# A 3x3 convolution on one core: cutting one input load into 112 and four times 4 partitions, and merging stores

## The chip, the core and the metric

The kernel runs on one core of one Trainium2 chip. The metric is device time in microseconds (us) of one execution: 126.62 us before the change, the median of 3 runs (126.53 to 126.68). Lower is better.

## The reference, cut to what matters

```python
x: (16, 64, 64, 64) float32        # batch, c_in, h, w
weight: (128, 64, 3, 3) float32    # c_out, c_in, kh, kw
x_pad = np.pad(x, ((0, 0), (0, 0), (1, 1), (1, 1)))
for b, co, ci, kh, kw:
    output[b, co] += weight[co, ci, kh, kw] * x_pad[b, ci, kh:kh+h, kw:kw+w]
```

The output is (16, 128, 64, 64) in float32. So 16.8 MB of x and 0.3 MB of weights come in from device memory (HBM), and 33.6 MB go out.

## The kernel before

The 16 images are worked on in eight pairs. A pair fills all 128 partitions of the on-chip memory (SBUF): two images of 64 input channels, each partition holding one 64x64 channel, 16 KB. In the output a partition is one of 128 output channels, and a pair has two images of 16 KB on each partition.

One tensor `homes` has nine such 16 KB slots on every partition. `X_HOME` says in which slot the x of each pair stands, `O_HOME` in which two neighbouring slots its output is built; slots are used again and again, so a slot can be written only when what it held before has been read. Pair 7, for example, builds its output in slots 2 and 3, and pair 4 built its own in slots 3 and 4.

Every pair is done in two halves `h`. In each half GpSimd (POOL) forms sums and differences of image rows in half precision (lines 106, 113, 119), ScalarE (ACT) casts rows (line 124), TensorE (PE) multiplies them with transformed weights into four accumulators (line 162), ACT copies three of these out (line 182), and VectorE (DVE) and ACT combine them into the pair's output slots (lines 229 to 232). POOL works two halves ahead of PE.

All transfers are issued by one engine, SyncE (SP), in the order of the program (`keep`), and each waits there for its inputs; a later one cannot pass it. The order before:

1. The weights (line 58), x of pair 0 in two pieces, of pair 1 and of pair 2 (line 63), then x of pairs 3 and 4 in one transfer (line 72).
2. After the second half of a pair, its output (`store`). Pairs in `BOTH` go out as one transfer of 2 images x 16 KB per partition (line 190), the others as one transfer per image (line 199). `FEW = 5, 1, 7` makes an exception for the second image of pair 5: its first 57 rows go out over all 128 partitions, its last 7 rows in one transfer of 124 partitions and one of 4.
3. After the first half of pairs 2, 3 and 4, the load of x of pairs 5, 6 and 7 (line 63).

That makes 24 transfers. Each uses one of eight semaphores in turn, and a transfer waits until the one that used its semaphore before has landed.

The functions the diff touches:

Of the kernel before, what the change touches and what calls it, by code (L numbers as in the profile page):

```python
# [15 lines left out]
def kernel(  # L16
# [12 lines left out]
    nc = tc.nc  # L29
    B, CI, H, W = x.shape  # L30
    CO = weight.shape[0]
# [4 lines left out]
    keep = tc.keep_in_program_order  # L36
    x_rows = x.rearrange("b c h w -> (b c) h w")
# [10 lines left out]

    X_HOME = [0, 1, 2, 7, 8, 2, 7, 8]
    O_HOME = [5, 3, 0, 5, 3, 0, 5, 2]  # L50
    BOTH = (0, 3, 6)
    FEW = 5, 1, 7
    NEXT_LOADS = {(2, 0): 5, (3, 0): 6, (4, 0): 7}
    homes = slots.tile([128, 9, H, W], F32)
    xs = [homes[:, k, :, :] for k in X_HOME]
# [1 line left out]
    w_raw = const.tile([CO, CI * 9], F32)  # L57
    keep(nc.sync.dma_start(w_raw, w_flat))

    def load(p, cuts=((0, H),)):  # L60
        for lo, hi in cuts:
            keep(
                nc.sync.dma_start(
                    xs[p][:, lo:hi, :], x_rows[128 * p : 128 * p + 128, lo:hi, :]
                )
            )

    load(0, ((0, 34), (34, H)))
    load(1)
    load(2)  # L70
    rows = x_rows[128 * 3 : 128 * 5, :, :].rearrange("(g p) h w -> p g h w", g=2)
    keep(nc.sync.dma_start(homes[:, 7:9, :, :], rows))

# [113 lines left out]
    def store(p, both):  # L187
        if p in BOTH:
            pair = out[2 * p : 2 * p + 2, :, :, :].rearrange("b c h w -> c b h w")
            keep(nc.sync.dma_start(pair, both))  # L190
            return
        for b2 in range(2):
            parts = [(0, CO, 0, H)]
            if (p, b2) == FEW[:2]:
                at = H - FEW[2]
                parts = [(0, CO, 0, at), (0, 124, at, H), (124, 4, at, H)]
            for c, n, lo, hi in parts:
                keep(
                    nc.sync.dma_start(
                        out[2 * p + b2, c : c + n, lo:hi, :], both[c : c + n, b2, lo:hi, :]  # L200
                    )
                )

    for n, (p, h) in enumerate(halves):
        if n + 2 < len(halves):
            tr[halves[n + 2]] = transforms(nc.gpsimd, *halves[n + 2])
        if h == 0:
            both = homes[:, O_HOME[p] : O_HOME[p] + 2, :, :]
# [24 lines left out]
        if h == 1:  # L233
            store(p, both)
# [32 lines left out]
```

## Time and profile before

| | |
|---|---|
| median of 3 runs | 126.62 us |
| the profiled execution's own time | 126.84 us |
| its span, first to last instruction | 125.0 us |
| busy: PE, ACT, POOL, DVE | 77%, 65%, 72%, 51% |
| time of the packets of SP's queue, as a share of 16 DMA engines' span | 96.6% |
| bytes moved, mean rate | 50.77 MB, 406 GB/s |
| output transfers of one image: issue to landing, median | 16.7 us |
| output transfers of two images: issue to landing, median | 21.2 us |

How to read it: "busy" is the time in which an engine executes something, over the whole span. The 16 DMA engines carry the transfers in packets; a packet here is one row of one partition, mostly 16 KB, and a last packet of 4 bytes raises the semaphore. The trace has a record of every packet (start, length, bytes, but not which of the 16 engines carried it) and of every increment of a semaphore, so that one can see when each engine's share of a transfer has landed. Times below that are not of the page count from the first instruction of the span.

### The profile page before, as it was taken

Reading aid. Unit: us, or ns where it says so; the run is one execution under the profiler, and the core shown is the slowest. Engines: PE = TensorE matmul, PEld = TensorE weight load, DVE = VectorE, ACT = ScalarE, POOL = GpSimd, SP = SyncE. Lnnn points to the kernel's source line nnn. Section 1 sums busy time; section 2 is a strip of 40 time slices with the busy share of each in tenths; the row PEclk is TensorE's granted clock in tenths of the full one; section 3 lists DMA queues with packets and bytes.
Section 4 is the critical chain, followed back from the end, with each engine's and each line's share of the span. In section 5 each row is a group of like instructions: output and inputs, shape, how many; then the busy total and the mean of one; then the engine's idle time right before and its main releaser. Section 6 shows DMA issues by size and latency. Waiting matters only on the chain.

```text
span 125.0 us, 2161 instructions
## 1 busy us (share of the span) xinstructions
PE 96.3 (77%) x873; PEld 48.3 (39%) x873; DVE 64.3 (51%) x56; ACT 81.5 (65%) x86; POOL 90.5 (72%) x52
## 2 busy tenths in 40 slices
PE   0339999999999999999999999999999991000000
PEld 0213455554545545554545555545545540000000
DVE  0199484655738393947557483939374664000000
ACT  4456569789897979797888989797978842000000
POOL 2209999999999999999999999999999500000000
PEclk9999999999999999999999999999999999555555
DMA  4999999999999999999999999999999999999991
GB/s 126 364 433 440 430 430 430 425 346 404 430 425 419 440 430 440 406 425 425 432 438 398 430 425 425 435 430 425 430 419 428 428 421 431 435 425 440 430 388 63
DMA packets 3826, 50.77 MB, mean 406 GB/s; under 512 B 360, under 2 KB 488, under 8 KB 744
## 3 DMA queue, kind: packets, MB, share of 16 engines
q1 hardware_dynamic: 3816, 50.63, 96.6%
q8 instruction: 7, 0.11, 0.3%
q14 instruction: 3, 0.02, 0.1%
HBM read 17.07 MB, written 33.55 MB: 405 GB/s over the span
## 4 chain that ended last, share of the span: by engine, by line
PE 77%; DVE 3%; DMA 3%; POOL 1%; ACT 0%; issue 0%; DVEq 0%
PE acc L162 76%; DMA w_raw<-in_weight_dram 3%; DVE homes L231 1%; DVE ss L106 1%; POOL w L78 1%; DVE th L133 0%; DVE Wt L134 0%; PE wp L95 0%; ACT g0h L131 0%; DVEq L134 0%
## 5 line engine op out<-in xcount | busy, mean ns | idle before, releaser
L162 PEld LDWEIGHTS <-Wt 64*128 64x128 f16 x864 | 47.4, 96 | 50.0 <-issue 4.4
L182 ACT COPY ut<-acc 128x1024 f32<-128x1024 f32 x48 | 45.7, 1021 | 5.5 <-PE acc L162 5.5
L162 PE MATMUL acc<-xh,Wt 64*128 64x504 f16 (+3 forms) x384 | 46.9, 376 | 0.0
L106 POOL TENSOR_TENSOR ss<-homes 128x1024 f16<-128x1024 f32 x15 | 35.3, 2352 | 5.0 <-DMA homes<-in_x_dram 5.0
L229 DVE TENSOR_TENSOR homes<-acc,ut 128x1024 f32<-128x1024 f32 x16 | 19.6, 1225 | 32.4 <-PE acc L162 30.2
L119 POOL TENSOR_TENSOR ee<-homes 128x1024 f16<-128x1024 f32 x15 | 35.4, 2359 | 0.0
L162 PE MATMUL acc<-ss,Wt 64*128 64x504 f16 (+1 forms) x192 | 24.8, 392 | 2.4 <-DVE ss L106 2.4
L162 PE MATMUL acc<-ee,Wt 64*128 64x504 f16 (+1 forms) x192 | 26.3, 377 | 0.0
L232 ACT COPY homes<-acc 128x1024 f32<-128x1024 f32 x16 | 16.2, 1013 | 12.7 <-PE acc L162 12.0
L231 DVE TENSOR_TENSOR homes<-ut,acc 128x1024 f32<-128x1024 f32 x16 | 19.5, 1221 | 2.0 <-PE acc L162 1.3
L113 POOL TENSOR_TENSOR dd<-homes 128x512 f16<-128x512 f32 x15 | 20.0, 1332 | 0.0
L230 DVE TENSOR_TENSOR homes<-acc,ut 128x1024 f32<-128x1024 f32 x16 | 19.4, 1215 | 0.0
L124 ACT CAST xh<-homes 128x1088 f16<-128x1088 f32 x16 | 17.9, 1120 | 0.0
L162 PE MATMUL acc<-dd,Wt 64*128 64x504 f16 (+1 forms) x96 | 13.9, 392 | 0.0
L95 PE MATMUL wp<-ident,w 128*128 128x128 f16 x9 | 1.1, 309 | 4.8 <-POOL w L78 4.8
L133 DVE SCALAR_TENSOR_TENSOR th<-wp,g0h 128x384 f32<-128x384 f32 x1 | 0.6, 557 | 5.8 <-ACT g0h L131 5.8
L119 DVE TENSOR_TENSOR ee<-homes 128x1024 f16<-128x1024 f32 x1 | 2.9, 2866 | 0.0
L95 PEld LDWEIGHTS <-w 128*128 128x128 f16 x9 | 0.9, 158 | 4.7 <-POOL w L78 4.7
L78 POOL CAST w<-w_raw 128x576 f16<-128x576 f32 x1 | 0.7, 662 | 2.7 <-DMA w_raw<-in_weight_dram 2.7
L79 ACT CAST w<-w_raw 128x576 f16<-128x576 f32 x1 | 0.7, 671 | 1.9 <-DMA w_raw<-in_weight_dram 1.9
L79 ACT ACT_TABLE_LOAD x1 | 1.3, 1283 | 0.7 <-PEq L251 0.7
L106 DVE TENSOR_TENSOR ss<-homes 128x1024 f16<-128x1024 f32 x1 | 1.2, 1224 | 0.0
(15 smaller groups left out, 5.7 us busy)
## 6 DMA issues: line engine op xcount, KB each, us to landing
out_dram<-homes SPq DMA_DIRECT2D x9, 2048.0 KB, 16.7
out_dram<-homes SPq DMA_DIRECT2D x3, 4096.0 KB, 21.2
homes<-in_x_dram SPq DMA_DIRECT2D x5, 2048.0 KB, 19.0
homes<-in_x_dram SPq DMA_DIRECT2D x1, 4096.0 KB, 28.0
out_dram<-homes SPq DMA_DIRECT2D x1, 1824.0 KB, 22.6
homes<-in_x_dram SPq DMA_DIRECT2D x1, 1088.0 KB, 5.8
homes<-in_x_dram SPq DMA_DIRECT2D x1, 960.0 KB, 7.8
w_raw<-in_weight_dram SPq DMA_DIRECT2D x1, 288.0 KB, 3.2
```

The costliest lines, as they stand in the source:

```text
L79: keep(nc.scalar.copy(w16[:, 1, :], w_raw))
L95: keep(nc.tensor.matmul(wps[kh][:, k * CO : k * CO + CO], w16[:, :, 3 * kh + k :: 9], ident))
L106: keep(eng.tensor_add(t, v[:, j : j + 16, 0, :], v[:, j : j + 16, 1, :]))
L113: keep(eng.tensor_sub(t, v[:, j : j + RB, 1, :], v[:, j : j + RB, 0, :]))
L119: keep(eng.tensor_sub(t, xs[p][:, r - 1 : r + 15, :], xs[p][:, r + 1 : r + 17, :]))
L124: keep(nc.scalar.copy(t, xs[p][:, C_ROW[h] : C_ROW[h] + 17, :]))
L162: nc.tensor.matmul(tiles[:, b2, lo:hi, c_lo:c_hi], Wt[p0 : p0 + 64, wi, kw, :], src[p0 : p0 + 64, first : last + 1 : step, c_lo + kw - 1 : ...
L182: keep(nc.scalar.copy(ut, tiles))
L229: keep(nc.vector.tensor_add(ov[:, :, jg : jg + RB, 1, :], pg2, ug))
L230: keep(nc.vector.tensor_add(ov[:, :, jf : jf + RB, 0, :], pf1, uy))
L231: keep(nc.vector.tensor_sub(ov[:, :, jf : jf + RB, 1, :], ux, pf2))
L232: keep(nc.scalar.copy(ov[:, :, jg : jg + RB, 0, :], pg1))
```

## The change

Three things are altered, and nothing in the computation.

- The load of pair 2 (`FEW = 2, 112, 4`) goes as one transfer of partitions 0 to 111 and four transfers of 4 partitions each (112 to 115, 116 to 119, 120 to 123, 124 to 127), instead of one of 128.
- The second image of pair 5 goes out whole, over 128 partitions; the transfers of 57 rows, of 7 rows on 124 partitions and of 7 rows on 4 partitions are gone.
- `BOTH` has pairs 0, 1, 3, 4 and 6 instead of 0, 3 and 6, so pairs 1 and 4 go out by one transfer each instead of two.

It stays at 24 transfers. The order of the instructions on PE, DVE, ACT and POOL is the same as before.

```diff
-    BOTH = (0, 3, 6)
-    FEW = 5, 1, 7
+    BOTH = (0, 1, 3, 4, 6)
+    FEW = 2, 112, 4
...
-    def load(p, cuts=((0, H),)):
+    def load(p, cuts=((0, H),), parts=((0, 128),)):
         for lo, hi in cuts:
-            keep(
-                nc.sync.dma_start(
-                    xs[p][:, lo:hi, :], x_rows[128 * p : 128 * p + 128, lo:hi, :]
+            for c, n in parts:
+                at = 128 * p + c
+                keep(
+                    nc.sync.dma_start(
+                        xs[p][c : c + n, lo:hi, :], x_rows[at : at + n, lo:hi, :]
+                    )
                 )
-            )
...
-    load(2)
+    few = [(c, FEW[2]) for c in range(FEW[1], 128, FEW[2])]
+    load(FEW[0], parts=[(0, FEW[1])] + few)
...
         for b2 in range(2):
-            parts = [(0, CO, 0, H)]
-            if (p, b2) == FEW[:2]:
-                at = H - FEW[2]
-                parts = [(0, CO, 0, at), (0, 124, at, H), (124, 4, at, H)]
-            for c, n, lo, hi in parts:
-                keep(
-                    nc.sync.dma_start(
-                        out[2 * p + b2, c : c + n, lo:hi, :], both[c : c + n, b2, lo:hi, :]
-                    )
-                )
+            keep(nc.sync.dma_start(out[2 * p + b2, :, :, :], both[:, b2, :, :]))
```

## The prediction

> **What bounds the kernel now.** I read the page's slices and DMA queues first, then the chain, SP's waits, the stretches, and at last the trace's records of single packets and of semaphore increments.
>
> ```profile
> span 125.0 us, 2161 instructions
> ...
> PE   0339999999999999999999999999999991000000
> ...
> DMA  4999999999999999999999999999999999999991
> GB/s 126 364 433 440 430 430 430 425 346 404 430 425 419 440 430 440 406 425 425 432 438 398 430 425 425 435 430 425 430 419 428 428 421 431 435 425 440 430 388 63
> ...
> q1 hardware_dynamic: 3816, 50.63, 96.6%
> ```
>
> All 16 DMA engines are busy from the second slice to the last, at about 430 GB/s; PE stops six slices earlier. The chain's view ends in the same place:
>
> ```profile
> 8.31 95.19 PE acc L162 x864
> 103.50 0.02 issue
> 103.52 1.22 DVE homes L231
> ```
>
> Computing is over at 104.74, and 20 us of stores remain. SP's timeline has the last two stores issued at 104.80, and its waits end in transfers (7.6 us the longest):
>
> ```profile
> 93.30 0.40 SPq L190 DMA_DIRECT2D out_dram<-homes  x1
> 104.80 1.92 SPq L199 DMA_DIRECT2D out_dram<-homes  x2
> ```
>
> ```profile
> SPq L262 <- DMA out_dram<-homes: 17.3, 3, 7.6
> ```
>
> So each DMA engine has a list that never runs dry, and the time is set by **the engine that ends last**. In the packet records a 16 KB packet takes 611 ns and the next on its engine starts 4 ns before its end: 0.607 us each. A 14592-byte packet (57 rows) takes 545, so 0.541; a 1792-byte one (7 rows) 74, one each 0.0706; a 4-byte end costs 0.006. The sixteen increments of the last store come from 120.87 to 124.22. The 4-row store of pair 5 has five increments, one at issue and four at the end, 103.78 to 104.57: it ran on four engines, and so did the 124-row one, with 31 rows each. I call these four A, the twelve others B. Following packets by end and start, A's last share lands at 123.90; the latest of all, 124.22, is a B that lost 1.5 us to an instruction fetch at 22.0 and more in the stretch at 25 to 28. After 124.22 come 0.83 us to the end of the span, and 1.79 from there to the execution's 126.84, which is 0.22 over the median: my sum is made against 126.84.
>
> **What the change moves between engines.**
>
> - The store of pair 5. B sends eight packets of 57 rows now (8 x 0.541 = 4.33) and eight whole ones after (4.86): +0.53. A had in addition 31 + 1 small ones (2.26) and two ends: 6.61 before, 4.87 after, -1.74.
> - The load of pair 2. 112 rows make 7 for each of 16 engines: B -0.61. A gets 7 + 4 packets instead of 8, and four more ends: 3 x 0.607 + 0.024 = +1.84. That 112 goes over 16 and 4 over four engines I take from 128, 124 and 4 in the trace before.
> - Two stores merged (pairs 1 and 4): two ends fewer on each engine, -0.012. Merging itself should cost nothing: in the increments, a store of two images took 9.72 us per engine (pair 6) and the two single ones of pair 7 9.71.
>
> By packets alone: B -0.09, the latest at 124.13; A +0.09, at 123.99. Were this all, the end would move by -0.09 us.
>
> **Queues and waits.** SP issues four more loads ahead of that of pairs 3 and 4, about 0.4 us each, and by the order of the semaphores that load also waits for pair 0's first piece, landed at 7.0. It is issued at about 7 instead of 3.29. The engines have work until pair 2 has landed (18.1 to 19.3), which hides it by 11 us; without that cover it would cost all of the 3.7. The removed stores stood at 83 to 85 on SP, which next waited until 93.3: nothing.
>
> Pair 2 is first read by POOL at 28.22, pair 3 at 39.98:
>
> ```profile
> 28.22 2.36 POOL L106 TENSOR_TENSOR ss<-homes 128x1024 f16<-128x1024 f32 x1
> ...
> 39.98 2.35 POOL L106 TENSOR_TENSOR ss<-homes 128x1024 f16<-128x1024 f32 x1
> ```
>
> A's rows of pair 2 come 1.8 us later, at 21.1, and pairs 3 and 4 (31.3 now) at most that much later: both hidden, by 7 us.
>
> One wait is new. Pair 7's first writes (slots 2 and 3) needed only pair 4's first image out of slot 3, landed at 90.73; with one transfer they need both, landed at 95.59 on the latest engine, less 0.6 in the new kernel:
>
> ```profile
> 95.41 1.23 DVE L229 TENSOR_TENSOR homes<-acc,ut 128x1024 f32<-128x1024 f32 x1 [2.17 <-PE acc L162]
> ```
>
> A, 92.2 to 93.2 there, comes at 95.0 at the latest. That is just in time; if A is later still, DVE waits, behind it two more DVE combines, then PE for its accumulators and the last store. That one has 6 us: the first engine reaches it at 111.2, and it is issued at 104.8. So the wait is hidden up to 6 us.
>
> **The cost that no row shows.** In the new load all four A engines write the same four neighbouring partitions at one time, four times over, while B already loads pairs 3 and 4 into the same partitions. Nearest is the 124-row store: its four engines read rows of partitions that B engines were reading too.
>
> ```profile
> 24.00:25.00 1.00, 1.00 (x12) 0.53 (x10) 0.17 (x1) 1.00 (x2) 1.00 (x2) 1.00 1.03 442
> 25.00:28.00 3.00, 3.00 (x32) 1.52 (x29) 1.74 (x2) 2.44 (x3) 3.00 (x2) 1.00 1.08 344
> ...
> 86.00:101.00 15.00, 15.00 (x145) 7.61 (x142) 8.53 (x9) 12.91 (x14) 12.77 (x7) 1.00 1.00 426
> 101.00:105.00 4.00, 2.48 (x24) 1.01 (x20) 3.57 (x3) 1.27 (x2) 0.00 (x0) 1.00 1.03 429
> ```
>
> The last column is the rate: 429 GB/s from 101 to 105, where those packets ran, 426 before it. All 128 small packets took 74 ns. So two engines at one group of partitions cost nothing, when they read. Four or five that write are not shown. Low end: they cost nothing either, 0. High end: one at a time, each of four packets takes four times as long, 4 x 3 x 0.607 = 7.3, or 4 x 4 x 0.607 = 9.7 with a B engine as the fifth. **I take what the row shows and no more**: two at full pace, so four get half each. In step that is 4 x 0.607 = 2.4 on A; A's ends lie 0.8 us apart in the trace, more than a packet, so part of it is lost to nothing: I take 1.7, an estimate. Seven-row shares of the 112 may meet in pairs as well, free by the same row.
>
> A then lands at 123.99 + 1.7 = 125.69, 1.47 behind 124.22: 126.84 + 1.47 = **128.3 us**, with its own range 127.2 to 129.7 (0.6 to 3.1 on A). DVE's new wait is then about 1.3 us, of the 6 hidden.
>
> **The rivals.**
>
> *One at a time.* If a group of partitions takes in only what one engine brings, A is late by 7.3 to 9.7: 131.3 to 133.7, so 126.84 + 7.1 to 9.5 = 133.9 to 136.3. A B engine whose partitions these are may lose four packet times, 2.4, and would still end before A. Against it: the 429 GB/s above. For it: nothing in this trace writes so. This is what the Trainium skill says, in SBUF — State Buffer, section "Door 1: The DMA port swizzle": partitions come in groups with one port each, 112 to 115 in one of them, and a transfer to partitions 0..3 alone was measured at 27.6 GB/s; by that page's figure 64 KB would take 2.4 us, four of them 9.5 instead of 2.4, an estimate. The trace, 429 GB/s, does not show that limit, for reads. Chance 0.25.
>
> *Free (not slower).* If writes are as free as the reads were, only the balance counts: the price is -0.09, and 126.75. It decides as soon as sharing costs A under 0.2 us. The stretch at 25 to 28 is the uncertainty: 344 GB/s against 430 is 3 x 86 / 430 = 0.6 us on every engine, in the last packets of the load of pairs 3 and 4; with A running later it may shrink or grow: 126.1 to 127.4. Chance 0.30: 0.13 faster, 0.12 the same, 0.05 slower.
>
> *The change does not do what it says.* If a 4-row load ran on one engine, this one would get 16 packets more, 9.7 us, and end past 133; the five increments of the 4-row store speak against it. With other mishaps, chance 0.07: 0.05 slower, 0.02 faster.
>
> **How the numbers follow.** Forecast 0.38, one at a time 0.25, free 0.30, others 0.07. Slower by over 0.2% (0.25 us, about what a measurement of this kernel can tell from no change): 0.38 + 0.25 + 0.05 + 0.05 = 0.73. Same 0.12. Faster 0.13 + 0.02 = 0.15. The range, 126.3 to 134.2, leaves out about half of "one at a time" (0.13) and the lowest of "free" (0.05).
>
> **What would show it.** Right: the 16 KB packets of the 4-row loads last about 1.0 us instead of 0.611, at 16 to 20 us, the rate dips there, and the four increments of each last 4-row load come about 3.5 us behind the others'; in the last store four engines land last, about 1.5 us behind B. One at a time: those packets last 2.4 us or more and the last slices show a quarter of the rate for 7 us. Free: all stay at 611 ns and the last store ends near 124.1. Wrong altogether: B engines late at the end, an empty DMA slice, or a computing end past 111.

## The result, and the profile after

The changed kernel takes **134.96 us**, the median of 6 runs (134.44 to 136.08), against 126.65 for the kernel before in the same comparison: 1.0647 times as long, 95% interval 1.0596 to 1.0697. It is slower, as forecast, but the forecast was 128.3 with a range up to 134.2, and the end moved for another reason than the forecast gave.

The page of the changed kernel, the 40 slices again (a slice is 3.3 us here), with the line of SP's queue:

```profile
span 133.3 us, 2166 instructions
...
PE   0359999999999999999999599938999694000000
...
DMA  4999999989999999999999999999999999999970
GB/s 141 381 451 433 260 280 143 123 241 428 413 433 428 437 428 425 428 437 418 433 415 450 408 437 423 433 428 437 423 428 433 433 423 428 433 433 433 433 310 34
...
q1 hardware_dynamic: 3664, 50.63, 96.0%
```

The two DMA rows have to be read together. The engines are "busy" all the time, as before; but in slices 5 to 9 the rate falls to 123 to 280 GB/s. A packet that waits counts as busy. From the tenth slice on everything is as it was, and the tail is much as before (310 and 34 in the last two slices, 388 and 63 before): no four engines are left working alone for long at the end. The same in stretches; the columns end with the granted clock, the DMA share and GB/s:

```profile
13.00:20.00 7.00, 7.00 (x70) 3.61 (x68) 4.05 (x4) 5.17 (x7) 7.00 (x5) 1.00 1.06 281
20.00:28.00 8.00, 8.00 (x78) 4.02 (x75) 5.65 (x6) 6.47 (x7) 7.72 (x4) 1.00 1.02 137
28.00:31.00 3.00, 3.00 (x32) 1.54 (x30) 1.03 (x1) 2.72 (x4) 0.66 (x1) 1.00 0.88 339
31.00:126.00 95.00, 74.63 (x672) 37.14 (x668) 46.02 (x39) 60.01 (x62) 69.93 (x36) 0.92 1.01 429
```

For the kernel before, the same first three stretches:

```profile
13.00:20.00 7.00, 7.00 (x64) 3.44 (x62) 3.61 (x4) 4.54 (x6) 7.00 (x5) 1.00 1.01 431
20.00:28.00 8.00, 8.00 (x78) 4.05 (x76) 5.32 (x5) 6.53 (x7) 8.00 (x5) 1.00 1.04 397
28.00:31.00 3.00, 3.00 (x32) 1.51 (x28) 1.84 (x2) 2.66 (x3) 3.00 (x3) 1.00 0.93 399
```

At 430 GB/s the 18 us from 13 to 31 would carry 18 x 430 = 7740 KB; the changed kernel carried 7 x 281 + 8 x 137 + 3 x 339 = 4080, a loss of 3660 / 430 = 8.5 us, and the kernel before lost 0.8 there. The difference, 7.7, is nearly all of the 8.3 by which the span grew. From 31 us to 126 the rate is 429.

In the packet records the 112-row load fills 13 to 20 us: its packets last about 1.0 us instead of 0.611, and it lands 6.85 us after the load before it, where 7 packets would take 4.25. From 20 to 28 us, while the 4-row loads run, 66 packets start, the median lasts 2.0 us, and **not one is under 1.09 us**. At most sixteen of them are packets of the 4-row loads; the others, mostly of the load of pairs 3 and 4, are as slow. So all sixteen engines wait, not only the four that carry the 4-row loads. The increments agree: pairs 3 and 4, loaded behind it, land 8.3 us later than before on the latest engine (39.6 instead of 31.3) and 7.6 later on the first (35.8 instead of 28.3).

The waits of the changed kernel show what it did to computing:

```profile
DVE homes L223 <- DMA out_dram<-homes: 13.0, 3, 5.6
...
POOL ss L109 <- DMA homes<-in_x_dram: 12.0, 4, 4.6
```

In the kernel before, DVE had no such wait, and POOL's was this:

```profile
POOL ss L106 <- DMA homes<-in_x_dram: 5.0, 1, 5.0
```

SP's timeline of the changed kernel has the last stores issued here:

```profile
112.74 1.39 SPq L196 DMA_DIRECT2D out_dram<-homes  x2
```

DVE waits for output slots whose stores come late, POOL for x, and computing ends 7.9 us later (the last stores are issued at 112.74, not 104.80). It costs nothing: the DMA engines are at 429 GB/s through all of it.

### The profile page after: what moved, and what is told of

It is laid out like the page before. It is cut to its first block, busy times and chain, and to the rows that moved or that the text cites. A ratio compares the mean times of both kernels' runs of the same rounds, so it can differ in the third digit from the quotient of the medians.

```text
span 133.3 us, 2166 instructions
## 1 busy us (share of the span) xinstructions
PE 98.8 (74%) x873; PEld 49.4 (37%) x873; DVE 63.5 (48%) x56; ACT 82.0 (61%) x86; POOL 90.6 (68%) x52
## 4 chain that ended last, share of the span: by engine, by line
DMA 45%; PE 29%; DVE 5%; issue 3%; ACT 1%; POOL 1%; DVEq 0%
DMA out_dram<-homes 42%; PE acc L165 29%; DVE homes L224 3%; DMA w_raw<-in_weight_dram 2%; ACT ut L185 1%; DVE homes L225 1%; DVE ss L109 1%; POOL w L81 1%; DVE th L136 0%; DVE Wt L137 0%; PE wp L98 0%; ACT g0h L134 0%; DVE homes L223 0%; DVEq L223 0%; DVEq L225 0%
## 5 line engine op out<-in xcount | busy, mean ns | idle before, releaser
L165 PEld LDWEIGHTS <-Wt 64*128 64x128 f16 x864 | 48.5, 96 | 57.0 <-issue 7.9
L185 ACT COPY ut<-acc 128x1024 f32<-128x1024 f32 x48 | 46.2, 1019 | 9.8 <-PE acc L165 9.4
L165 PE MATMUL acc<-ss,Wt 64*128 64x504 f16 (+1 forms) x192 | 26.2, 400 | 8.1 <-DVE homes L223 4.6
L165 PE MATMUL acc<-dd,Wt 64*128 64x504 f16 (+1 forms) x96 | 14.6, 408 | 0.0
```

What stands on the lines that cost most here:

```text
L165: nc.tensor.matmul(tiles[:, b2, lo:hi, c_lo:c_hi], Wt[p0 : p0 + 64, wi, kw, :], src[p0 : p0 + 64, first : last + 1 : step, c_lo + kw - 1 : ...
L185: keep(nc.scalar.copy(ut, tiles))
```

## The experiments

A time below is the median of 2 to 12 runs; in brackets stand its ratio to the kernel before, measured beside it, and the 95% interval of that ratio.

### Which side is crowded, and is it the size of the transfers?

Three theories of the 4-row loads: N, neighbouring partitions of SBUF take in only what one engine brings, and those who wait hold up the others; H, the rows in device memory are too near; S, small transfers are slow. Three edits of the four loads, on the changed kernel:

```diff
-    load(FEW[0], parts=[(0, FEW[1])] + few)
+    load(FEW[0], parts=[(0, FEW[1])])
+    for c in range(FEW[1], FEW[1] + 4):
+        keep(nc.sync.dma_start(xs[2][c:128:4, :, :], x_rows[256 + c : 384 : 4, :, :]))
```

> The changed kernel, but each of the four 4-row loads takes every fourth partition (112, 116, 120, 124 and so on) instead of four neighbours, from the matching rows of x. Theory N (neighbouring partitions take in only what one engine brings, and engines that wait there hold the others up): the four engines of a transfer now write four different groups, so the stretch at 20 to 29 us, about 6 us lost on every engine, shrinks to under 1.5; the 112-row load still loses its 2.7. Time 129 to 130.5. Theory H (the rows read from device memory are too near each other): also gone, 129 to 130.5. Theory S (four small transfers are slow by themselves): no change, 134.5 to 135.5.

The second, with only the memory side spread, was `xs[2][c : c + 4]` from `x_rows[256 + 112 + k : 384 : 4]`:

> The changed kernel, but each 4-row load writes four neighbouring partitions (112 to 115 and so on) from every fourth row of x, so that only the memory side is spread out. It puts 16 rows of pair 2 into other partitions than the reference has them, so those channels are mixed up. Theory N: no change, 134.5 to 135.5, the 4-row packets still take about 2 us. Theory H: the loss of the 4-row loads is gone, 129 to 130.5. Theory S: 134.5 to 135.5.

The third, with only the SBUF side spread, was `xs[2][112 + k : 128 : 4]` from four neighbouring rows:

> The mirror of the run before: each 4-row load reads four neighbouring rows of x and writes every fourth partition, so that only the on-chip side is spread out. 16 rows of pair 2 land in other partitions than the reference has them. Theory N: 129 to 130.5, as with both sides spread. Theory H: no change, 134.5 to 135.5. Theory S: 134.5 to 135.5.

Measured: both sides spread 131.31 us (ratio 1.0347, 1.0318 to 1.0377); memory side only 135.25 (1.0655, 1.0585 to 1.0725); SBUF side only 131.30 (1.0344, 1.0306 to 1.0382). The stretches, first with both sides spread:

```profile
20.00:28.00 8.00, 8.00 (x78) 4.09 (x76) 5.65 (x6) 6.48 (x7) 8.00 (x5) 1.00 0.99 283
```

memory side only:

```profile
13.00:20.00 7.00, 7.00 (x69) 3.62 (x67) 4.90 (x5) 5.59 (x6) 7.00 (x5) 1.00 1.07 300
20.00:28.00 8.00, 8.00 (x78) 4.13 (x76) 5.65 (x5) 6.40 (x7) 7.67 (x4) 1.00 0.97 133
```

then SBUF side only:

```profile
13.00:20.00 7.00, 7.00 (x70) 3.58 (x68) 4.89 (x5) 5.63 (x6) 7.00 (x5) 1.00 1.07 276
20.00:28.00 8.00, 8.00 (x78) 4.01 (x76) 5.65 (x5) 6.26 (x7) 8.00 (x5) 1.00 0.95 270
```

From 20 to 28 us the rates are 283, 133 and 270 GB/s: it is the partitions that make the difference, not the rows in device memory. H falls, S does not explain it, and N stands in its main point: what is crowded is a place in SBUF. The spread ones came out 0.8 above the upper end of what N was given. Their packets tell why: from 20 to 25 us they last 1.24 to 1.26 us in the median, and the shortest with both sides spread 0.885; the pace is half, for all engines. The likely reason is that four engines at four groups, where other engines load pairs 3 and 4, make two at a group. That is a reading: no record says which engine is at which partition.

### The cut alone, without shifting work

```diff
-    load(FEW[0], parts=[(0, FEW[1])] + few)
+    load(2)
...
+    load(FEW[0], parts=[(0, 112), (112, 16)])
...
+    load(2, parts=[(0, 64), (64, 64)])
```

Each added line is a kernel of its own: the whole load, 112 and 16, and halves.

> The changed kernel with the load of pair 2 in one transfer of 128 partitions: the merged stores and the whole store of pair 5 alone, with no shifting of work between engines. By the packet arithmetic the latest B engine has 8 whole packets instead of 8 of 57 rows in the store of pair 5, +0.53 against the kernel before, and the four A engines end 1.7 earlier: 127.1, 0.4% slower than before. All theories of the 4-row loads agree here. If merging the stores of pairs 1 and 4 costs something (the wait of pair 7 for both images of pair 4), it is over 127.4.

> The changed kernel with the last 16 partitions of pair 2 in one transfer of 16, over 16 engines, one row each, instead of four of 4. Theory N: 16 engines write the four groups of those 16 partitions, four engines each, so one packet takes 1.7 to 2.4 us on every engine instead of 0.61; with 2.7 lost in the 112-row load and no shifting of work to four engines (127.1 for that) it gives 131 to 131.7. If only the 4-row form is slow, and 112 rows lose their 2.7 by themselves: 129.8. If both are harmless: 127.1.

> Merged stores, whole store of pair 5, and the load of pair 2 cut into two transfers of 64 partitions. No 112, no 4. Theory N: half the partitions have half the groups, so each 64-row load goes at half the rate, 4.9 us instead of 2.4 on every engine: 127.1 + 4.9 = 132, with packets of 1.2 us at 13 to 23. The Trainium skill says the same, in SBUF — State Buffer, section Door 1: The DMA port swizzle, where 64 partitions reach 8 of 16 ports. Theories H and S: 127.1 to 127.4.

The whole load takes 127.71 us (1.0054, 1.0027 to 1.0081), where packet arithmetic said 0.4% slower (the kernel before took 126.86 in this comparison). 112 and 16 take 131.80 (1.0384, 1.0343 to 1.0425), just over the 131 to 131.7 of theory N; halves 132.18 (1.0413, 1.0383 to 1.0444), where 132 was expected. Halves have neither a 112 nor a small transfer in them, and the stretches are at half the rate:

```profile
13.00:18.00 5.00, 5.00 (x46) 2.51 (x44) 3.53 (x3) 2.65 (x4) 5.00 (x3) 1.00 1.08 233
18.00:23.00 5.00, 5.00 (x50) 2.51 (x48) 2.82 (x4) 4.32 (x5) 5.00 (x4) 1.00 1.05 223
```

The same two transfers of 64, cut into even and odd partitions instead of halves:

```diff
+    for c in range(2):
+        keep(nc.sync.dma_start(xs[2][c:128:2, :, :], x_rows[256 + c : 384 : 2, :, :]))
```

> Merged stores, whole store of pair 5, the load of pair 2 cut into two transfers of 64, the even partitions and the odd ones, so that each reaches all partition groups (the cut into halves cost 5 us). If it is the number of groups reached that counts and engines spread over them: 127.3 to 127.7, packets of 611 ns. If any cut to 64 partitions costs the same (each engine's rows then span the groups of two, in step): 130 to 132.5.

127.55 us (1.0033, 1.0003 to 1.0063), the time of the whole load:

```profile
13.00:18.00 5.00, 5.00 (x50) 2.56 (x48) 3.58 (x3) 3.56 (x4) 5.00 (x3) 1.00 1.04 442
18.00:23.00 5.00, 5.00 (x52) 2.54 (x48) 3.58 (x3) 4.09 (x6) 5.00 (x4) 1.00 0.98 416
```

442 and 416 against 233 and 223, with the same bytes in as many transfers: the cut itself costs nothing, the cut into halves costs half the rate. (The even and odd cut also takes every second row of device memory; spreading that side alone had changed nothing for the 4-row loads.) This is the rule of the Trainium skill, SBUF — State Buffer, section "Door 1: The DMA port swizzle" (0..63 reach 8 of 16 ports), and these two runs agree with it.

### Does one crowded load hold up everybody?

One more transfer beside whole ones, on the kernel before; its four rows are read by nothing:

```diff
     load(2)
+    keep(nc.sync.dma_start(homes[112:116, 3, :, :], x_rows[368:372, :, :]))
```

> The kernel before with one transfer added: between the loads of pair 2 and of pairs 3 and 4, four rows of x go once more into partitions 112 to 115 of a slot that is still free (nothing reads them). Packet arithmetic alone: four engines +0.61, which puts them 0.3 behind the latest: 127.1. Theory B (a crowded group holds up all engines): about 16 packets of some 2 us at 18 to 22, every engine loses 1.3 to 1.8: 128 to 129. Theory O (only those who write there wait): four or five long packets, the other engines at 611 ns; the four engines end 2 us later: 128.7 to 129. Times may agree, the packet lengths tell.

128.93 us (1.0124, 1.0078 to 1.0170). The kernel with the extra load, then the kernel before, in the same stretches:

```profile
18.00:21.50 3.50, 3.50 (x37) 1.82 (x34) 2.35 (x2) 2.88 (x4) 3.50 (x3) 1.00 0.99 197
21.50:25.00 3.50, 3.50 (x36) 1.79 (x34) 1.28 (x2) 3.22 (x4) 3.50 (x3) 1.00 1.00 421
25.00:28.00 3.00, 3.00 (x32) 1.53 (x28) 2.90 (x3) 2.14 (x3) 3.00 (x2) 1.00 1.02 437
```

```profile
18.00:21.50 3.50, 3.50 (x38) 1.78 (x34) 1.49 (x2) 3.50 (x4) 3.50 (x3) 1.00 0.99 426
21.50:25.00 3.50, 3.50 (x36) 1.76 (x34) 2.51 (x3) 2.59 (x4) 3.50 (x3) 1.00 1.01 426
25.00:28.00 3.00, 3.00 (x32) 1.52 (x29) 1.74 (x2) 2.44 (x3) 3.00 (x2) 1.00 1.08 344
```

64 KB in one group of partitions pulled the whole load from 426 to 197 GB/s for 3.5 us, on average 1.9 us of every engine's time; even the first engine to land pairs 3 and 4 does so 1.6 us later than before (29.83 instead of 28.27). 32 of the 39 packets of 16 KB that start from 18 to 21.1 us last over 0.8 us, up to 2.3; those that start from 19 to 20 all last over 1.59. Theory B holds: everybody waits. (The loss at 25 to 28, 344 GB/s before, is gone in this run, which gives 0.6 back.) The Trainium skill's page "DMA: Bandwidth & Descriptors", section "Back-pressure in remote DMA", tells of a saturated SBUF port that clogs engines sharing the path. That is said of transfers between cores; this run shows all engines slowed on a load from memory, but does not show by which path.

### Why did the 124-row store mislead?

The prediction had read from it that two engines at a group cost nothing. The same cuts on the store of pair 5's second image, with the load of pair 2 whole; `cut` is (0, 64), (64, 64) in the first kernel, 112 and four times 4 in the second, and one piece for every other image:

```diff
-            keep(nc.sync.dma_start(out[2 * p + b2, :, :, :], both[:, b2, :, :]))
+            for c, n in cut:
+                keep(nc.sync.dma_start(out[2 * p + b2, c : c + n, :, :], both[c : c + n, b2, :, :]))
```

> Merged stores, whole load of pair 2, and the store of the second image of pair 5 cut into two transfers of 64 partitions: the same cut on the side that reads partitions. If reading is as free as the 124-row store of the kernel before showed (429 GB/s): 127.1 to 127.3, and no packet over 0.64 us there. If reading is limited like writing: 132.

> The cut of the change, 112 and four times 4 neighbouring partitions, on the store of pair 5's second image instead of on the load of pair 2; the load is whole. If reading neighbouring partitions is free, only the balance counts: the latest B engine -0.61, A +1.84 against a whole store, that is about -0.09 and +0.1 against the kernel before: 126.5 to 126.8. If four engines that read four neighbouring partitions share one engine's worth: 133 to 136.

Halves 132.84 us (1.0466, 1.0426 to 1.0505), 112 and four times 4 132.77 (1.0446, 1.0402 to 1.0489), just under the 133 to 136 given for shared engines. Reading is limited too. The store in halves, and the kernel before:

```profile
97.00:105.00 8.00, 6.11 (x54) 2.94 (x54) 6.11 (x6) 4.36 (x5) 1.45 (x1) 1.00 1.05 313
```

```profile
97.00:105.00 8.00, 6.48 (x62) 3.03 (x58) 5.56 (x5) 4.87 (x5) 1.77 (x1) 1.00 1.01 427
```

It looks different in the records: of 168 packets of 16 KB that start at 97 to 106 us, 87 keep their 611 ns and 11 last up to 0.64 us; 70 are longer, up to 2.6 us. As on the load, the engines hardly stand still meanwhile (DMA share 1.05).

With 112 and four times 4 the end looks different too. The page's slices (3.3 us each):

```profile
GB/s 142 355 442 447 417 427 437 422 368 408 452 408 447 422 413 420 417 437 430 422 403 425 412 437 427 417 442 417 432 422 338 308 343 408 412 452 398 248 94 25
```

In the last store eleven engines land by 125.12 us, as all do in the run with everything whole (by 125.07); five land from 126.79 to 131.04. So on this store a few engines pay most, and a long slow tail, the sign of the rival "one at a time", is there, unlike on the load. Either way the limit is there when partitions are read too, so the side was not the reason. Two more kernels, from the one before, asked for the size:

```diff
-                parts = [(0, CO, 0, at), (0, 124, at, H), (124, 4, at, H)]
+                parts = [(0, CO, 0, at), (0, 64, at, H), (64, 64, at, H)]
```

> The kernel before, but the 7-row strip of pair 5's second image goes as 64 and 64 partitions over 16 engines instead of 124 and 4 over four. It asks why the 124-row strip was free although reading crowded partitions costs 5 us with 16 KB packets. Theory L (short packets do not crowd): all packets 74 ns, time as without shifting, 127.3 to 127.8. Theory G (the 124 rows were spread so that they met nobody for long): with half the groups for 16 engines the 1792-byte packets last about 140 ns, or stand apart, and every engine loses about 0.6 us: 127.9 to 128.4.

```diff
-    FEW = 5, 1, 7
+    FEW = 5, 1, 28
```

> The kernel before with a strip of 28 rows instead of 7: packets of 7168 bytes on 124 partitions, 31 for each of four engines. By packet times the four engines end 4.6 us later than before and alone set the end: 131 to 131.6, if the 7168-byte packets take 0.27 us each (theory G: the 124 rows meet nobody for long, whatever their length). Theory L (only short packets are free): many of them last longer or stand apart, and the time is 133 or more.

The strip in halves takes 127.36 us (1.0031, 1.0013 to 1.0049): all 128 packets last 74 ns, and the stretch stays at 427 GB/s. The 28-row strip takes 140.97 (1.1101, 1.1064 to 1.1137), some 9.5 over what its packets alone would give. 61 of its 128 packets last over 300 ns instead of 272, up to 1086, and the four engines that carry them end at 129.4 to 138.2, the others by 122.8. The strip in halves where it runs, and then the 28-row strip, which runs later:

```profile
97.00:105.00 8.00, 5.33 (x51) 2.49 (x46) 4.47 (x4) 3.88 (x5) 1.65 (x1) 1.00 1.02 427
```

```profile
105.00:112.00 7.00, 0.00 (x0) 0.00 (x0) 0.00 (x0) 0.00 (x0) 0.00 (x0) 0.68 0.99 372
```

Theory L holds: on 124 partitions over four engines, packets of 1792 bytes all took 74 ns, and of those of 7168 bytes nearly half were slowed. Where between the two it begins, and why, was not tried. On the load even the short strip is not free:

```diff
-    load(FEW[0], parts=[(0, FEW[1])] + few)
+    load(2, ((0, 57),))
+    load(2, ((57, H),), [(0, 124), (124, 4)])
```

> The shifting of the kernel before, moved to the load of pair 2 in its old form: 57 rows on 128 partitions, then 7 rows on 124 partitions and on 4; the stores are those of the change. Theory W (any write that meets another engine's group slows all engines): while the strip runs, three of four of its packets meet a group in use, so all engines go at half pace for 2.3 to 4.5 us: 128.5 to 130. If the strip is as free on the load as it is on the store: 126.5 to 127.1, which would be the change's idea without its cost.

128.00 us (1.0089, 1.0062 to 1.0116), below the 128.5 to 130 of theory W but well clear of free. 83 of the 128 short packets last over 80 ns, up to 206, and 16 KB packets around them up to 1.2 us:

```profile
17.00:22.00 5.00, 5.00 (x50) 2.52 (x48) 2.99 (x3) 4.10 (x6) 5.00 (x3) 1.00 1.04 307
```

### The merged stores, and a try at something better

```diff
-    BOTH = (0, 3, 6)
+    BOTH = (0, 1, 3, 4, 6)
```

> The kernel before with one edit: pairs 1 and 4 stored by one transfer each. By the increments a store of two images takes as long as two of one image, so 126.6 to 126.9, the same within 0.2%. If the wait of pair 7 for both images of pair 4 (or anything else of the merging) reaches the end, 0.3% or more slower; the whole-load run, 0.2 above the 127.5 that packet arithmetic gives on the reference of its own chip, leaves room for that.

126.96 us (1.0010, 0.9987 to 1.0033): no difference that can be told.

```diff
-    rows = x_rows[128 * 3 : 128 * 5, :, :].rearrange("(g p) h w -> p g h w", g=2)
-    keep(nc.sync.dma_start(homes[:, 7:9, :, :], rows))
+    load(3)
+    load(4)
```

> The kernel before with the load of pairs 3 and 4 in two transfers of 128 partitions instead of one. If the 0.6 us that every engine loses at 25 to 28 comes from that transfer's form, 126.2; if not, 126.7 to 126.9 as before.

127.28 us (1.0020, 0.9986 to 1.0053): the loss at 25 to 28 us is there as before (344 GB/s), packets up to 2.3 us, so the form of that transfer is not its cause. No version was found that is faster than the kernel before.

## Why the prediction was wrong, point by point

- **What bounds the kernel: right.** The lists of the DMA engines set the end. Computing came 7.9 us later without any effect, though the late loads were not "hidden, by 7 us": pair 2 was complete at 30.13, where POOL had read it from 28.22 before, and POOL's waits for x grew from 5.0 to 12.0 us. The prediction had named a computing end past 111 as a sign that it was wrong altogether, and that sign was badly chosen, since all lists had grown as much.
- **The balance between A and B: right as far as it was seen, and too small to matter.** The increments show the 112 rows on sixteen engines and each 4-row load on four. The run with the whole load, which leaves the shifting out, is 0.54% slower than before, against 0.4% by packet arithmetic; the part of the sum for the load of pair 2 lies under the crowding and was not seen alone.
- **Merging costs nothing: right** (1.0010). The new wait of pair 7 is hidden.
- **"I take what the row shows and no more": the step that failed.** Two at full pace, so four at half, and 1.7 us, on A alone. The row was the 124-row store at 429 GB/s. It showed that packets of 1792 bytes can be read so; taken for a rule on engines that share partitions it does not hold for 16 KB packets, read (halves: 4.7% slower than the kernel before) or written (4.1%, with everything whole 0.5%). The 4-row loads' packets lasted 2.0 us in the median, not the forecast's 1.0; and with both sides spread, where by the reading above two were at a group, all packets took twice as long. In the forecast's own terms, A's last share was to land at 123.99 + 1.7; it landed at 132.51, 8.5 behind 123.99.
- **The sharing was put on the wrong engines.** The prediction, and its rival "one at a time", let A alone wait and B go on. On a load everybody waits: one extra 4-row load cost all sixteen 1.9 us on average. A, the four engines of the 4-row loads, does end behind B, as forecast: followed from pairs 3 and 4 (it lands there at 38.40 to 39.59, B by 37.66), four of the last five increments, 130.64 to 132.51, are A's. But B itself, which was to end by 124.13, has its last shares at 128.08 to 129.94 and one later; "B engines late at the end" was one of the prediction's own signs of being wrong altogether, and it came. So the end came by luck near what the rival gave (133.9 to 136.3; measured 134.96), without its sign, a tail at a quarter of the rate: four 4-row packets took the four engines about 8.6 us (from 20.2 to 21.5, where the 112 rows landed, to 28.7 to 30.1), the others needed 15.7 us instead of 9.7 for the 16 packets beside them, and all were late together.
- **"Seven-row shares of the 112 may meet in pairs as well, free by the same row": wrong.** The 112 rows cost 2.6 us on every engine (6.85 instead of 4.25), before the first 4-row load had started. That the shares meet is the likely reason, but it is not shown: no run cut 112 rows in another way.
- **The rule of the Trainium skill's page (SBUF — State Buffer, "Door 1") was weighed too lightly.** The rival beside it had a chance of 0.25 against a row that was another size of packet. Halves against even and odd partitions is the pair of runs that bears it out here.

## What to carry to other kernels

When a transfer is cut by partitions, ask which partitions the engines are at together: loading 112 partitions cost a third of the rate here (281 GB/s against 431), halves one half, blocks of four beside other loads two thirds, even and odd partitions nothing. On a load the price is paid by all engines, so a few rows moved to balance the ends by 0.1 us can cost 8. A row of the trace that shows something free shows it for its own packet size: before it carries a forecast, look whether another row has the size in question, and if none has, keep the rule that speaks against it at its full weight.

## What the runs showed of the hardware that was not expected

- One 64 KB load into four neighbouring partitions slows all sixteen engines (426 to 197 GB/s for 3.5 us). The busy share stays at 0.99 while it happens, which hides it from whoever reads the DMA row alone.
- On stores crowding looks otherwise: about half of the packets keep 611 ns while others last up to 2.6 us (halves), and with 112 and four times 4 five of sixteen engines end up to 6 us behind the rest (131.04 against 125.12).
- The loss of the kernel before at 25 to 28 us (344 GB/s) goes away in runs whose loads were slowed ahead of it (437 GB/s with the extra 4-row load). What causes it stayed open.
